# Recurrence of a two-layer hybrid decoder: paired level products, lanes that follow by an event, a shorter stated norm latency

## The chip, the cores and the metric

The kernel runs on one core of a Trainium2 chip. The core has five engines that matter here: TensorE (PE in the profile, with PEld for its weight loads), VectorE (DVE), ScalarE (ACT), GpSimd (POOL) and SyncE (SP), which issues the DMA transfers. Each engine works through its own instructions in order; semaphores let one wait for another. The metric is the device time of one execution in microseconds, as the median of several runs.

## The reference

Two decoder layers over 256 tokens of width 1024 in float32. Each layer adds to `x`, in this order, half a SwiGLU feed-forward block, a mixer, a cross attention over 256 memory tokens and another half feed-forward block, each behind an RMS norm. The mixer has two groups of heads side by side:

```python
z = h @ w_in                       # HGRN2 q|f|i|g, FoX q|k|v, forget logits
# HGRN2, 4 heads of 128: a gated linear recurrence
S_t = diag(f_t) S_{t-1} + (1 - f_t) i_t^T ;  o_t = S_t^T q_t
o_h = rms_norm(o_h, out_norm_w) * silu(g)
# FoX, 8 heads of 64: causal softmax attention with decaying bias
s = q k^T / 8 + (c_t - c_s),  c = cumsum(log sigmoid(ff + b))
o_f = softmax(s) v
x = x + concat(o_h, o_f) @ w_out
```

## The kernel before

**Precision and the large products.** Float32 results are built from three products of a fast 32-bit kind: high times high, high times low, low times high (`mm3`, lines 455 to 458). Activations and weights are split for that into a high and a low part: ScalarE casts the high part (`whi`, lines 159 and 163), VectorE subtracts it from the original for the low part (`wlo`, lines 160 and 164; `xfl`, `oTl`, `mfl`, line 383). Weights stream in by DMA in a fixed list of pieces of up to 1 MB (`raw`, three buffers), so TensorE's large matmuls, ScalarE's casts and VectorE's subtractions run side by side through the whole kernel. The large matmuls write the tiles `acc`, in four PSUM buffers; all small groups write tiles of one pool of four PSUM buffers (`smp`: ad, al, pc, mt, ax, ho, fs, fpt, fpv, hot, pt), taken in rotation.

**What sets the order.** The Python code of the kernel is a set of generators that `drive` runs against a virtual clock while the program is written. A generator that yields a number has used so much TensorE time; a tuple of one number means "not before so much later"; an `Event` means "not before it has been fired". The constants `LAT_...` state how long the other engines will take before TensorE's next step of that generator has its operands. So TensorE's order is fixed when the program is built, by these stated latencies; if one is too short, TensorE waits in order on a semaphore and everything behind it waits too. On ScalarE, VectorE and GpSimd a scheduler orders the instructions with priorities; some steps are raised (`high_priority`).

**The recurrence** (`hgrn`, lines 783 to 878) is worked out by doubling. Query and key (both [128 features, 4 heads, 256 tokens]; `q`, `qf = q*f`, `k`) meet first on the diagonal (`ad`), then on seven levels with blocks of 1, 2, 4 ... 64 tokens (`al`). A level multiplies k by qf in blocks (32 pairs of 32x32, 16 of 32x32 or 8 of 64x64; one pair shows as two matmuls in the trace). VectorE then takes the decays of the halves into the second half of qf (line 819) and the first half of k (line 821), both in place, works out the totals for the next level (line 825), and picks the level's entries out of PSUM into `Ac` by a mask (line 832). Levels 5 and 6 and the finished `Ac` are copied by ScalarE into the score matrix `A` (lines 829 and 836). After the last level come one product between the two halves of the tokens (`ax`, copied by ScalarE to `AX`, line 845), the outputs `ho` for the two token tiles (lines 855 and 856), and a norm per head: squares on ScalarE (line 863), sums on VectorE (line 865), a power on GpSimd (line 867), the scaling on VectorE (line 869, to `AX` for the first token tile and to `oh` for the second), and their transposes on TensorE (`hot`, line 875), split into `oTh` and `oTl`.

**The lanes.** Two generators `fox_lane` take two pairs of heads each. Per pair: `fox_stack` builds split queries and keys with the bias stacked in (`fqs`, `fks`, ScalarE's casts on lines 946 to 948), TensorE makes the scores (`fs`, line 967), VectorE adds the causal mask and takes the maximum, ScalarE the exponential (line 929), TensorE transposes the result (`fpt`, line 985), ScalarE copies it (`ppT`, line 988), and TensorE multiplies with v (`fpv`, lines 998 to 1000). The second lane's first pair is held 2.8 us of virtual time behind the first lane's.

**Around them** the main generator keeps writing large matmuls: the projections for FoX, the memory keys and values (`mfh`, `mfl`), then the output projection with the tiles `vc`, and the norm behind the mixer (`hn`, its inverse root on line 357, transposes `pt` on line 376), whose latency is stated as `LAT_X`.

Of the kernel before, what the change touches and what calls it, by code (L numbers as in the profile page):

```python
# [13 lines left out]
ALU = mybir.AluOpType  # L14
# [3 lines left out]
P = 128  # L18
# [16 lines left out]
TAIL = 6  # L35
HP = 100
LA_D, LA_S = 3, 1
LAT_NORM, LAT_X = 5.5, 6.5
LAT_LVL, LAT_AX, LAT_HN = 4.0, 1.5, 5.2
LAT_FS, LAT_FT, LAT_CQ, LAT_CS, LAT_CT = 7.0, 3.5, 2.6, 5.6, 3.0  # L40
LAT_Q, LAT_G1, LAT_G2, LAT_M = 5.0, 9.0, 2.0, 18.0
LAT_MEM = 42.0
LAT_FK, LAT_LANE = 6.5, 2.8

OFF_Q, OFF_F, OFF_I, OFF_G = 0, 512, 1024, 1536
OFF_FQ, OFF_FK, OFF_FV = 2048, 2560, 3072
# [3 lines left out]
def hymba_kernel(  # L50
# [6 lines left out]
    nc = tc.nc  # L57
# [26 lines left out]
    def smp(name="smp"):  # L84
        return pss.tile([P, 512], F32, name=nm(name), tag="smp")
# [328 lines left out]
    def spawn(gen):  # L414
        tasks.append([gen, clock[0], None])
# [365 lines left out]
    def hgrn(q, f, k, v, gw, oT, masks, ready, done):  # L781
        yield ready
        masks, eye = masks
        A2 = s4([P, NT, 4, P], F32, "A")
        A = [A2[:, t] for t in range(NT)]
        nc.gpsimd.memset(A2, 0.0)
        Ac = sm.tile([P, 8, 32], F32, name=nm("Ac"), tag="Ac", bufs=1)
        qf = s4([P, 4, S], F32, "qf")
        nc.vector.tensor_tensor(out=qf, in0=q, in1=f, op=ALU.mult)

        def blocks(ps, rhs, hb, step):

            for t in range(NT):
                for h in range(4):
                    c0 = (4 * t + h) * hb
                    for s0 in range(0, P, hb + step):
                        a = t * P + s0
                        nc.tensor.matmul(ps[s0:s0 + hb, c0:c0 + hb], lhsT=k[:, h, a:a + hb],  # L798
                                         rhs=rhs[:, h, a + step:a + step + hb], start=True, stop=True)

        ps = smp("ad")
        blocks(ps, q, 32, 0)
        nc.vector.tensor_tensor(out=Ac, in0=ps[:, 0:256].rearrange("p (g t) -> p g t", g=8),
                                in1=eye.unsqueeze(1).to_broadcast([P, 8, 32]), op=ALU.mult)
        yield 1.3
        tots = s4([P, 1024], F32, "tots")
        tot = f.rearrange("p h t -> p (h t)")
        qflat = qf.rearrange("p h t -> p (h t)")
        kflat = k.rearrange("p h t -> p (h t)")
        for lv in range(7):  # L810
            hb = 1 << lv
            ps = smp("al")
            blocks(ps, qf, max(32, hb), hb if lv >= 5 else 0)
            nb = 4 * S // (2 * hb)
            tv = tot.rearrange("p (b two) -> p b two", two=2)
            qv = qflat.rearrange("p (b two j) -> p b two j", two=2, j=hb)
            kv = kflat.rearrange("p (b two j) -> p b two j", two=2, j=hb)
            with tc.high_priority(offset=HP):
                nc.vector.tensor_tensor(out=qv[:, :, 1, :], in0=qv[:, :, 1, :],
                                        in1=tv[:, :, 0:1].to_broadcast([P, nb, hb]), op=ALU.mult)  # L820
                nc.vector.tensor_tensor(out=kv[:, :, 0, :], in0=kv[:, :, 0, :],
                                        in1=tv[:, :, 1:2].to_broadcast([P, nb, hb]), op=ALU.mult)
                if lv < 6:
                    nt_ = tots[:, 1024 - 2 * nb:1024 - nb]
                    nc.vector.tensor_tensor(out=nt_, in0=tv[:, :, 0], in1=tv[:, :, 1], op=ALU.mult)
                    tot = nt_
            if lv >= 5:
                for s0 in range(0, P, 2 * hb):
                    nc.scalar.copy(out=A2[s0:s0 + hb, :, :, s0 + hb:s0 + 2 * hb],
                                   in_=ps[s0:s0 + hb, 0:8 * hb].rearrange("p (t h j) -> p t h j", t=NT, h=4))  # L830
            else:
                nc.vector.copy_predicated(Ac, masks[:, lv, :].unsqueeze(1).to_broadcast([P, 8, 32]),
                                          ps[:, 0:256].rearrange("p (g t) -> p g t", g=8))
            if lv == 4:
                for s0 in range(0, P, 32):
                    nc.scalar.copy(out=A2[s0:s0 + 32, :, :, s0:s0 + 32],
                                   in_=Ac[s0:s0 + 32].rearrange("p (t h) j -> p t h j", t=NT))
            yield 1.3 if lv < 5 else 0.8
            yield (LAT_LVL,)
        ps = smp("ax")  # L840
        for h in range(4):
            nc.tensor.matmul(ps[:, h * P:(h + 1) * P], lhsT=k[:, h, 0:P], rhs=qf[:, h, P:S], start=True, stop=True)
        AX2 = s4([P, 2, 4, P], F32, "AX")
        AX_ = AX2[:, 0]
        nc.scalar.copy(out=AX_, in_=ps.rearrange("p (h t) -> p h t", h=4))
        yield 4 * 0.213
        yield (LAT_AX,)
        oT.alloc(0)
        ohs = []
        for t in range(NT):  # L850
            po = smp("ho")
            for h in range(4):
                o = po[:, h * P:(h + 1) * P]
                if t == 1:
                    nc.tensor.matmul(o, lhsT=AX_[:, h, :], rhs=v[:, 0, h * P:(h + 1) * P], start=True, stop=False)
                nc.tensor.matmul(o, lhsT=A[t][:, h, :], rhs=v[:, t, h * P:(h + 1) * P], start=t == 0, stop=True)
            yield (4 + 4 * t) * 0.213
            oh_ = AX2[:, 1] if t == 0 else s4([P, 4, P], F32, "oh")
            ohs.append(oh_)
            pv = po.rearrange("p (h e) -> p h e", h=4)  # L860
            ss = small(4, "hss")
            for h in range(4):
                nc.scalar.activation(oh_[:, h, :], pv[:, h, :], AF.Square, scale=float(P) ** -0.5,
                                     accum_out=ss[:, h:h + 1])
            nc.vector.tensor_scalar(out=ss, in0=ss, scalar1=EPS, scalar2=None, op0=ALU.add)
            rs = small(4, "hrs")
            nc.gpsimd.tensor_tensor(out=rs, in0=ss, in1=neghalf, op=ALU.pow)  # L867
            for h in range(4):
                nc.vector.scalar_tensor_tensor(out=oh_[:, h, :], in0=pv[:, h, :], scalar=rs[:, h:h + 1],
                                               in1=gw[:, t, h * P:(h + 1) * P], op0=ALU.mult, op1=ALU.mult)  # L870
        yield (LAT_HN,)
        for t in range(NT):
            pt = smp("hot")
            for h in range(4):
                nc.tensor.transpose(pt[:, h * P:(h + 1) * P], ohs[t][:, h, :], ident)
            sl = slice(t * P, (t + 1) * P)
            put_split(oT.h[0][:, :, sl], oT.l[0][:, :, sl], pt.rearrange("p (k t) -> p k t", k=4))
            yield 4 * T1
        done.fire(1.6)
# [74 lines left out]
                                    scalar2=None, op0=ALU.mult)  # L954
        return qs, ks

    def fox_lane(lane, fq, fk, fv, L_, R_, oT, cmask, oh, ready, done):
        yield ready
        for pr in (lane, lane + 2):
            qs, ks = fox_stack(pr, fq, fk, L_, R_, oh)  # L960
            yield (LAT_FK + LAT_LANE * (pr == 1),)
            prs = []
            for sub in range(2):
                ps = smp("fs")
                for t, o, n in SEGS:
                    for j in range(2):
                        nc.tensor.matmul(ps[:, o:o + n], lhsT=qs[:, j, sub, t * P:(t + 1) * P], rhs=ks[:, j, sub, 0:n],
                                         start=j == 0, stop=j == 1)
                yield 0.44
                pr_ = pp()  # L970
                prs.append(pr_)
                mx = small(2, "fmx")
                for t, o, n in SEGS:
                    nc.vector.tensor_tensor_reduce(out=pr_[:, o:o + n], in0=ps[:, o:o + n], in1=cmask[:, S - n:S],
                                                   scale=1.0, scalar=-3.0e38, op0=ALU.add, op1=ALU.max,
                                                   accum_out=mx[:, t:t + 1])
                nmx = small(2, "fnm")
                nc.vector.tensor_scalar(out=nmx, in0=mx, scalar1=-1.0, scalar2=None, op0=ALU.mult)
                softmax(pr_, nmx, 1.0, [(t, pr_[:, o:o + n], pr_[:, o:o + n]) for t, o, n in SEGS])
            yield (LAT_FS,)  # L980
            pTs = []
            for sub in range(2):
# [9 lines left out]
            for sub in range(2):  # L992
                h = 2 * pr + sub
# [16 lines left out]
    def mixer(cur, l, consts, nxt_w):  # L1010
# [57 lines left out]
            nc.scalar.copy(out=fv[:, t, 0:260], in_=ps[t][:, 0:260])  # L1068
        oT.alloc(1)
        ev_p = [Event() for _ in range(4)]  # L1070
        for lane in range(2):
            spawn(fox_lane(lane, fq, fk, fv, L_, R_, oT, cmask, oh, ev_g, ev_p))
        kc = [[s4([P, 4, S], F32R, "kc") for _ in range(2)] for _ in range(2)]
        yield ev_m
        for c in range(2):
# [180 lines left out]
```

## Time and profile before

| | before |
|---|---|
| median of 3 runs | 1209.25 us (1209.22 to 1209.48) |
| profiled execution | 1209.23 us |
| span of its instructions | 1207.4 us |
| granted TensorE clock | 0.999 |
| busy: TensorE / VectorE / ScalarE / GpSimd | 99% / 64% / 54% / 3% of the span |
| DMA, mean over the span | 181 GB/s |

The profile is one execution. Busy shares are taken of the span, which leaves out 1.8 us at the execution's ends. Matmuls are pipelined: their recorded durations overlap, so the distance between two starts says what one costs, and the idle times in the list of waits say where TensorE had nothing to do. In the timeline's rows the bracket gives the idle time before the row and what ended it.

### The profile page before, as it was taken

How to read it: one execution, taken by the hardware profiler on the slowest of the kernel's cores; microseconds unless marked ns; L12 is line 12 of the kernel's file. 1: busy time of each engine (PE TensorE's matmuls, PEld its weight loads, DVE VectorE, ACT ScalarE, POOL GpSimd, SP SyncE). 2: the span in 40 equal slices, each digit the busy share in tenths (PEclk: the TensorE clock that was granted, in tenths of full speed). 3: DMA queues.
4: the chain of work that ended last, by engine and by line, in shares of the span. 5: the costliest groups of instructions: out<-in, count | busy, mean ns of one | idle time of the engine just before them, and what ended most of it. 6: DMA issues, size and time to landing. Idle time of an engine off the chain costs nothing.

```text
span 1207.4 us, 21487 instructions
## 1 busy us (share of the span) xinstructions
PE 1194.0 (99%) x8989; PEld 1095.0 (91%) x8989; DVE 769.1 (64%) x1194; ACT 651.2 (54%) x1022; POOL 36.7 (3%) x50
## 2 busy tenths in 40 slices
PE   9999999999999999999999999999999999999997
PEld 7999888999889889998889998889988898999986
DVE  6866647578866675565474565476787766555643
ACT  7565735568854454444354454266686555444532
POOL 0000000001000000000000000000110000000000
PEclk9999999999999999999999999999999999999999
DMA  8655755544544374566474566464445533555750
GB/s 300 217 195 179 273 183 174 168 136 140 180 152 175 105 262 154 195 212 207 140 261 141 209 210 209 140 227 159 149 150 174 191 128 136 194 192 175 245 174 36
DMA packets 100001, 218.66 MB, mean 181 GB/s; under 512 B 4128, under 2 KB 16704, under 8 KB 99904
## 3 DMA queue, kind: packets, MB, share of 16 engines
q1 hardware_dynamic: 99744, 217.03, 53.1%
q8 instruction: 70, 1.15, 0.4%
q10 hardware_dynamic: 160, 0.27, 0.1%
q14 instruction: 27, 0.22, 0.1%
HBM read 216.23 MB, written 1.05 MB: 180 GB/s over the span
## 4 chain that ended last, share of the span: by engine, by line
PE 88%; DVE 5%; ACT 3%; issue 2%; POOL 1%; DMA 0%; POOLq 0%; ACTq 0%
PE acc L456 27%; PE acc L458 27%; PE acc L457 27%; DVE wlo L164 1%; DVE wlo L160 1%; ACT whi L163 1%; PE acc L521 1%; PE pt L376 1%; POOL rs L357 1%; PE al L798 1%; DVE xfl L383 0%; ACT pp L929 0%; POOL hrs L867 0%; PE cpo L457 0%; PE cpo L456 0%
## 5 line engine op out<-in xcount | busy, mean ns | idle before, releaser
L160 DVE TENSOR_TENSOR wlo<-raw,whi 128x1024 fp32r<-128x1024 f32 (+1 forms) x332 | 389.5, 1197 | 251.8 <-ACT whi L159 243.3
L159 ACT CAST whi<-raw 128x1024 fp32r<-128x1024 f32 (+1 forms) x332 | 331.9, 1029 | 256.6 <-PE acc L458 144.7
L456 PE MATMUL acc<-xfh,whi 128*128 128x256 f32 x1536 | 425.5, 277 | 1.0 <-issue 1.0
L457 PE MATMUL acc<-xfl,whi 128*128 128x256 f32 x1536 | 424.3, 276 | 0.7 <-DVE xfl L383 0.7
L458 PE MATMUL acc<-xfh,wlo 128*128 128x256 f32 x1536 | 424.1, 276 | 0.0
L457 PEld LDWEIGHTS acc<-xfl,whi 128*128 128x128 f32 x1536 | 288.3, 188 | 2.5 <-DVE xfl L383 1.1
L456 PEld LDWEIGHTS acc<-xfh,whi 128*128 128x128 f32 x1536 | 288.4, 188 | 0.8
L458 PEld LDWEIGHTS acc<-xfh,wlo 128*128 128x128 f32 x1536 | 288.3, 188 | 0.0
L456 PE MATMUL acc<-whi,hth 128*128 128x512 f32 (+1 forms) x352 | 137.0, 389 | 0.0
L458 PE MATMUL acc<-whi,htl 128*128 128x512 f32 (+1 forms) x352 | 136.4, 387 | 0.0
L457 PE MATMUL acc<-wlo,hth 128*128 128x512 f32 (+1 forms) x352 | 136.3, 387 | 0.0
L456 PE MATMUL acc<-whi,xfh 128*128 128x512 f32 (+1 forms) x240 | 87.5, 365 | 0.0
L458 PE MATMUL acc<-whi,xfl 128*128 128x512 f32 (+1 forms) x240 | 86.9, 362 | 0.0
L457 PE MATMUL acc<-wlo,xfh 128*128 128x512 f32 (+1 forms) x240 | 86.6, 361 | 0.0
L458 PEld LDWEIGHTS acc<-whi,htl 128*128 128x128 f32 x352 | 66.1, 188 | 13.6
L456 PEld LDWEIGHTS acc<-whi,hth 128*128 128x128 f32 x352 | 66.1, 188 | 13.3
L457 PEld LDWEIGHTS acc<-wlo,hth 128*128 128x128 f32 x352 | 66.1, 188 | 13.3
L164 DVE SCALAR_TENSOR_TENSOR wlo<-raw,g,whi 128x512 fp32r<-128x512 f32 (+1 forms) x96 | 62.1, 702 | 19.7 <-ACT whi L163 19.7
L163 ACT ACTIVATE whi<-raw,g 128x512 fp32r<-128x512 f32 (+1 forms) x96 | 58.3, 677 | 18.0 <-PE acc L457 15.0
L458 PEld LDWEIGHTS acc<-whi,xfl 128*128 128x128 f32 x240 | 45.1, 188 | 7.2
L457 PEld LDWEIGHTS acc<-wlo,xfh 128*128 128x128 f32 x240 | 45.1, 188 | 6.9
L456 PEld LDWEIGHTS acc<-whi,xfh 128*128 128x128 f32 x240 | 45.1, 188 | 6.8
(274 smaller groups left out, 1498.2 us busy)
## 6 DMA issues: line engine op xcount, KB each, us to landing
raw<-in_ffn_w_down_dram SPq DMA_DIRECT2D x44, 1024.0 KB, 4.9
raw<-in_ffn_w_up_dram SPq DMA_DIRECT2D x40, 1024.0 KB, 5.5
raw<-in_ffn_w_gate_dram SPq DMA_DIRECT2D x38, 1024.0 KB, 5.2
raw<-in_w_in_dram SPq DMA_DIRECT2D x24, 1024.0 KB, 5.3
raw<-in_cross_wk_dram SPq DMA_DIRECT2D x8, 1024.0 KB, 5.6
raw<-in_cross_wv_dram SPq DMA_DIRECT2D x8, 1024.0 KB, 5.3
raw<-in_w_out_dram SPq DMA_DIRECT2D x8, 1024.0 KB, 5.0
raw<-in_cross_wq_dram SPq DMA_DIRECT2D x8, 1024.0 KB, 5.1
```

The lines of the kernel that those rows point to most:

```text
L159: nc.scalar.copy(out=hi, in_=sl)
L160: nc.vector.tensor_tensor(out=lo, in0=sl, in1=hi.bitcast(F32), op=ALU.subtract)
L163: nc.scalar.mul(hi, sl, g)
L164: nc.vector.scalar_tensor_tensor(out=lo, in0=sl, scalar=g, in1=hi.bitcast(F32), op0=ALU.mult, op1=ALU.subtract)
L357: nc.gpsimd.tensor_tensor(out=rs, in0=ms, in1=neghalf[:, 0:1], op=ALU.pow)
L376: nc.tensor.transpose(pt[:, j * P:(j + 1) * P], hn[:, kt * P:(kt + 1) * P], ident)
L456: nc.tensor.matmul(ps, lhsT=lh, rhs=rh, start=start, stop=False)
L457: nc.tensor.matmul(ps, lhsT=lh, rhs=rl, start=False, stop=False)
L458: nc.tensor.matmul(ps, lhsT=ll, rhs=rh, start=False, stop=stop)
L521: nc.tensor.matmul(psa_[t], lhsT=x, rhs=w, start=kt == 0 and which == 0, stop=kt == KT - 1 and which == 1)
L798: nc.tensor.matmul(ps[s0:s0 + hb, c0:c0 + hb], lhsT=k[:, h, a:a + hb], rhs=rhs[:, h, a + step:a + step + hb], start=True, stop=True)
```

## The change

- Level 1 and level 3 of the recurrence are held: their products are issued together with those of level 2 and level 4, as one burst into two halves of one PSUM tile. The held level's operands must stay as they are until then, so its updated query and key go to a spare pair of tiles (`q` and `f`, which are done with by then, and back). VectorE writes the changed halves there, and ScalarE copies the unchanged halves: two more copies at each held level.
- Level 0's products go into the second half of the diagonal's tile. The two groups stood next to each other before.
- The wait after a held level is stated as `LAT_LV2` = 7.0, and level 0 and 2 lead straight on to the held level's updates.
- The second lane no longer follows by a fixed wait. The first lane fires an event behind the softmax of its first pair, with a latency of 1.9, and the second lane waits for it before its scores.
- `LAT_X`, stated for the norm behind the mixer, goes from 6.5 to 5.3.

```diff
-LAT_NORM, LAT_X = 5.5, 6.5
+LAT_NORM, LAT_X = 5.5, 5.3
+LAT_LV2 = 7.0
...
-LAT_FK, LAT_LANE = 6.5, 2.8
+LAT_FK, LAT_LANE = 6.5, 1.9
...
-        def blocks(ps, rhs, hb, step):
+        def blocks(ps, k, rhs, hb, step):
...
         ps = smp("ad")
-        blocks(ps, q, 32, 0)
...
-        yield 1.3
+        blocks(ps, k, q, 32, 0)
...
+        old, spare = [], (q, f)
         for lv in range(7):
             hb = 1 << lv
-            ps = smp("al")
-            blocks(ps, qf, max(32, hb), hb if lv >= 5 else 0)
+            held = lv in (1, 3)
+            pend = [] if held else old + [(lv, k, qf)]
+            lvs = []
+            if lv and not held:
+                ps = smp("al")
+            for l_, k_, q_ in pend:
+                part = ps[:, 256:512] if l_ in (0, 2, 4) else ps
+                blocks(part, k_, q_, max(32, 1 << l_), hb if lv >= 5 else 0)
+                lvs.append((l_, part))
...
+            qv, kv = halves(qf), halves(k)
+            if held:
+                old, (qf, k), spare = [(lv, k, qf)], spare, (qf, k)
+            else:
+                old = []
+            qn, kn = halves(qf), halves(k)
             with tc.high_priority(offset=HP):
-                nc.vector.tensor_tensor(out=qv[:, :, 1, :], in0=qv[:, :, 1, :],
+                nc.vector.tensor_tensor(out=qn[:, :, 1, :], in0=qv[:, :, 1, :],
                                         in1=tv[:, :, 0:1].to_broadcast([P, nb, hb]), op=ALU.mult)
-                nc.vector.tensor_tensor(out=kv[:, :, 0, :], in0=kv[:, :, 0, :],
+                nc.vector.tensor_tensor(out=kn[:, :, 0, :], in0=kv[:, :, 0, :],
                                         in1=tv[:, :, 1:2].to_broadcast([P, nb, hb]), op=ALU.mult)
+                if held:
+                    nc.scalar.copy(out=qn[:, :, 0, :], in_=qv[:, :, 0, :])
+                    nc.scalar.copy(out=kn[:, :, 1, :], in_=kv[:, :, 1, :])
...
-            yield 1.3 if lv < 5 else 0.8
-            yield (LAT_LVL,)
+            if held:
+                yield (LAT_LV2,)
+            else:
+                yield 0.7 * (len(lvs) + (lv == 0)) if lv < 5 else 0.8
+                yield (LAT_LVL if lv not in (0, 2) else 0.0,)
...
     def fox_lane(lane, ..., ready, done, ahead):
...
-            yield (LAT_FK + LAT_LANE * (pr == 1),)
+            yield (LAT_FK,)
+            if pr == 1:
+                yield ahead
...
+            if pr == 0:
+                ahead.fire(LAT_LANE)
             yield (LAT_FS,)
```

More of the change, by code (lines that the diff above doesn't have):

```diff
@@ L801, in hgrn @@
         ps = smp("ad")
-        blocks(ps, q, 32, 0)
-        nc.vector.tensor_tensor(out=Ac, in0=ps[:, 0:256].rearrange("p (g t) -> p g t", g=8),
-                                in1=eye.unsqueeze(1).to_broadcast([P, 8, 32]), op=ALU.mult)
-        yield 1.3
+        blocks(ps, k, q, 32, 0)
         tots = s4([P, 1024], F32, "tots")
         tot = f.rearrange("p h t -> p (h t)")
-        qflat = qf.rearrange("p h t -> p (h t)")
-        kflat = k.rearrange("p h t -> p (h t)")
+        old, spare = [], (q, f)
@@ L814, in hgrn, with halves @@
             nb = 4 * S // (2 * hb)
             tv = tot.rearrange("p (b two) -> p b two", two=2)
-            qv = qflat.rearrange("p (b two j) -> p b two j", two=2, j=hb)
-            kv = kflat.rearrange("p (b two j) -> p b two j", two=2, j=hb)
+            def halves(x):
+                return x.rearrange("p h t -> p (h t)").rearrange("p (b two j) -> p b two j", two=2, j=hb)
+            qv, kv = halves(qf), halves(k)
[3 more added lines that the diff above has]
+                old = []
@@ L831, in hgrn @@
             else:
-                nc.vector.copy_predicated(Ac, masks[:, lv, :].unsqueeze(1).to_broadcast([P, 8, 32]),
-                                          ps[:, 0:256].rearrange("p (g t) -> p g t", g=8))
+                if lv == 0:
+                    nc.vector.tensor_tensor(out=Ac, in0=ps[:, 0:256].rearrange("p (g t) -> p g t", g=8),
+                                            in1=eye.unsqueeze(1).to_broadcast([P, 8, 32]), op=ALU.mult)
+                for l_, part in lvs:
+                    nc.vector.copy_predicated(Ac, masks[:, l_, :].unsqueeze(1).to_broadcast([P, 8, 32]),
+                                              part[:, 0:256].rearrange("p (g t) -> p g t", g=8))
             if lv == 4:
@@ L955, in fox_stack, with fox_lane @@
         return qs, ks
-    def fox_lane(lane, fq, fk, fv, L_, R_, oT, cmask, oh, ready, done):
+    def fox_lane(lane, fq, fk, fv, L_, R_, oT, cmask, oh, ready, done, ahead):
         yield ready
@@ L1070, in mixer @@
         ev_p = [Event() for _ in range(4)]
+        ahead = Event()
         for lane in range(2):
-            spawn(fox_lane(lane, fq, fk, fv, L_, R_, oT, cmask, oh, ev_g, ev_p))
+            spawn(fox_lane(lane, fq, fk, fv, L_, R_, oT, cmask, oh, ev_g, ev_p, ahead))
         kc = [[s4([P, 4, S], F32R, "kc") for _ in range(2)] for _ in range(2)]
```

## The prediction

> **What bounds the kernel now.** I read the profile's page first, then the list of TensorE's waits, then the timeline of TensorE through both mixers, and last the timelines of ScalarE and VectorE beside it. The page says which engine sets the time (first its busy line, then the chain that ended last, by engine):
>
> ```profile
> PE 1194.0 (99%) x8989; PEld 1095.0 (91%) x8989; DVE 769.1 (64%) x1194; ACT 651.2 (54%) x1022; POOL 36.7 (3%) x50
> ...
> PE 88%; DVE 5%; ACT 3%; issue 2%; POOL 1%; DMA 0%; POOLq 0%; ACTq 0%
> ```
>
> TensorE is busy for 1194.0 of a span of 1207.4 us. VectorE (64%) and ScalarE (54%) have room on the average. So time can come from only two places: holes in TensorE's row, and the price of each small group of matmuls that stands between the large ones. The profiled execution took 1209.23 us, 1.8 us more than its span; the median of the runs is 1209.25, so sums made on the span carry over.
>
> The holes, from the list of TensorE's waits (us in total, times, longest):
>
> ```profile
> PE fs L967 <- DVE AX L869: 1.0, 1, 1.0
> PE acc L456 <- issue: 1.0, 1, 1.0
> PE fpt L985 <- DVE oTl L383: 0.8, 1, 0.8
> PE acc L457 <- DVE xfl L383: 0.7, 2, 0.4
> PE acc L458 <- DVE wlo L164: 0.5, 1, 0.5
> PE pt L376 <- DVE hn L370: 0.4, 2, 0.2
> PE fpv L998 <- ACT ppT L988: 0.3, 1, 0.3
> ```
>
> These seven add to 4.7 us. Five of them (fs, issue, fpt, wlo, fpv: 3.6) lie inside a mixer, and xfl (0.7) right behind each. That is about all that better placing can win.
>
> The price of a small group is read at the recurrence of layer 1, on TensorE's timeline (start, us, engine, line, operation; "x64" is one level's burst):
>
> ```profile
> 242.43 0.28 PE L458 MATMUL acc<-whi,xfl 128*128 128x260 f32 x1
> 242.64 0.73 PE L798 MATMUL ad<-hq,kk 128*32 128x32 f32 x62
> ...
> 243.23 0.74 PE L798 MATMUL al<-qf,kk 128*32 128x32 f32 x62
> 243.90 0.39 PE L456 MATMUL acc<-xfh,whi 128*128 128x256 f32 x1
> 244.12 0.28 PE L457 MATMUL acc<-xfl,whi 128*128 128x256 f32 x1
> ...
> 244.92 0.28 PE L458 MATMUL acc<-xfh,wlo 128*128 128x256 f32 x1
> 246.21 0.28 PE L456 MATMUL acc<-xfh,whi 128*128 128x256 f32 x1 [1.01 <-issue]
> 246.32 0.28 PE L457 MATMUL acc<-xfl,whi 128*128 128x256 f32 x1
> ...
> 249.62 0.28 PE L458 MATMUL acc<-xfh,wlo 128*128 128x256 f32 x1
> 249.83 0.76 PE L798 MATMUL al<-qf,kk 128*32 128x32 f32 x64
> 250.52 0.39 PE L456 MATMUL acc<-xfh,whi 128*128 128x256 f32 x1
> 250.75 0.28 PE L457 MATMUL acc<-xfl,whi 128*128 128x256 f32 x1
> ```
>
> Large matmuls of 256 columns start 0.115 us apart. A level alone takes from 249.62 to 250.75, 1.13 us with two such steps in it, so 0.90. "ad" and the first level back to back take from 242.43 to 244.12, 1.69, less 0.23 is 1.46. The second burst thus costs 0.56 instead of 0.90: **a join saves 0.34, and each break of two neighbours costs about as much**.
>
> **The change part by part.** *Joins.* The small groups on TensorE in layer 1, in program order, before (ad and al are the bursts of the levels, pc the gates' prefix sum, mt the transposes of mem; large matmuls stand at each mark):
>
> ```order
> L798 MATMUL ad_2631<-hq_2429,kk_2298 32x32 x32
> L798 MATMUL al_2666<-qf_2629,kk_2298 32x32 x32
> ...
> L798 MATMUL al_2779<-qf_2629,kk_2298 32x32 x32
> ...
> L908 MATMUL pc_2854<-tri,lf_2740 128x256 x2
> L798 MATMUL al_2857<-qf_2629,kk_2298 32x32 x32
> L1120 MATMUL mt_2894<-ident,mem_1992 128x128 x4
> ```
>
> and with the change:
>
> ```order
> L799 MATMUL ad_2631<-hq_2429,kk_2298 32x32 x32
> L799 MATMUL ad_2631<-qf_2629,kk_2298 32x32 x32
> ...
> L799 MATMUL al_2812<-qf_2629,kk_2298 32x32 x32
> L799 MATMUL al_2812<-hq_2429,fg_2297 32x32 x32
> ...
> L799 MATMUL al_2988<-hq_2429,fg_2297 32x32 x32
> L799 MATMUL al_2988<-qf_2629,kk_2298 32x32 x32
> L1149 MATMUL mt_3062<-ident,mem_2003 128x128 x4
> ```
>
> "ad" and level 0 were neighbours already. Levels 1 and 2 join (0.34) and 3 and 4 join (0.34), but level 2 had stood beside pc and mt, and leaves them (one break back). Net one join a layer: 2 x -0.34 = **-0.7**. Nothing (0) would be the end if bursts in two halves of one tile cost as two; 2 x -0.68 = -1.4 the other.
>
> *Copies.* A held level writes its updated operands to spare tiles, which adds two ScalarE copies of 128x512, at 2 levels in 2 layers 8 copies. The nearest row, and ScalarE's room where they fall in layer 1 (the window's busy time of each engine):
>
> ```profile
> L1124 ACT COPY mem_t<-mt 128x512 f32<-128x512 f32 x4 | 2.4, 602 | 2.3 <-DVE mfl L383 2.3
> 246.00:262.00 16.00, 15.79 (x304) 15.02 (x304) 11.42 (x26) 8.41 (x16) 0.00 (x0) 1.00 0.20 52
> ```
>
> ScalarE is idle for 7.6 of those 16 us, so 4 x 0.6 = 2.4 are hidden there behind the large matmuls: **0**. Without that cover each pair would hold a burst back by 1.2, 4.8 in all. VectorE's updates are as large as they were.
>
> *Norm behind the mixer.* The stated latency falls from 6.5 to 5.3, so its transposes, and the split that VectorE does from them, are issued earlier. The wait to be won (layer 1; VectorE, then TensorE):
>
> ```profile
> 359.95 5.76 DVE L160 TENSOR_TENSOR wlo<-raw,whi 128x1024 fp32r<-128x1024 f32 x5
> 365.62 1.28 DVE L383 TENSOR_TENSOR xfl<-pt,xfh 128x512 fp32r<-128x512 f32 x2
> 366.36 0.39 PE L457 MATMUL acc<-xfl,whi 128*128 128x256 f32 x1 [0.34 <-DVE xfl L383]
> ```
>
> xfl stands in VectorE's queue behind five weight splits; asked for 1.2 us earlier it passes one. I take the 0.7 of both layers as gone: **-0.7**. Not more, and not below 0 to +0.7, should the transposes now wait for hn as they do for 0.4 above.
>
> *Lanes, layer 2.* Before, ho and the scores of both lanes (fs) stood in one block:
>
> ```profile
> 884.92 1.17 PE L967 MATMUL fs<-fks,fqs 128*128 128x128 f32 x8
> 887.14 1.28 PE L967 MATMUL fs<-fks,fqs 128*128 128x128 f32 x8 [1.05 <-DVE AX L869]
> ...
> 896.92 1.14 PE L985 MATMUL fpt<-ident,pp 128*128 128x128 f32 x6 [0.81 <-DVE oTl L383]
> ```
>
> Now 12 large matmuls follow ho, then lane 0, then 18 more, then lane 1 (TensorE, layer 2, end of the recurrence):
>
> ```order
> L880 MATMUL ho_9555<-hv_8329,A_8836 128x128
> ...
> L993 MATMUL fs_9589<-fks_9451,fqs_9450 128x128 x2
> ...
> L993 MATMUL fs_9643<-fks_9467,fqs_9466 128x128 x2
> L993 MATMUL fs_9643<-fks_9467,fqs_9466 128x256 x2
> L993 MATMUL fs_9661<-fks_9467,fqs_9466 128x128 x2
> ...
> L899 MATMUL hot_9685<-ident,AX_9519 128x128 x4
> L899 MATMUL hot_9692<-ident,oh_9564 128x128 x4
> ```
>
> So fs of lane 1 comes 12 x 0.115 + 1.0 + 18 x 0.115 = 4.5 us after ho, past the VectorE step that frees its bank (AX): -1.05. fpt (0.81) and wlo (0.5) move apart in the same way: -1.3. Small excesses beside these (in the two blocks quoted, 0.1 to 0.3 each): -0.6. Against it stand four breaks (ho|fs, fs|fs, and two where the products with v no longer pair) at 0.34: +1.3. And a new wait: the second half of lane 1 (fs_9661) takes the bank of ho's second half, freed only when VectorE has read it for oh, which I put at 7.6 us behind ho against 7.1 + 0.5 for the matmul; with ScalarE's copy of AX up to 0.7 late, +1.1 (0 to 2). Layer 2: -1.05 - 1.3 - 0.6 + 1.3 + 1.1 = **-0.6**.
>
> *Lanes, layer 1.* The rows of before (group rows of ScalarE's casts for the lanes; then single rows of three engines at the end of the recurrence):
>
> ```profile
> L946 ACT CAST fqs<-fq 64x512 fp32r<-64x512 f32 x16 | 9.9, 616 | 0.2
> L948 ACT CAST fks<-fk 64x256 fp32r<-64x256 f32 x16 | 6.5, 405 | 0.4
> 282.83 1.05 PE L842 MATMUL ax<-qf,kk 128*128 128x128 f32 x8
> 285.75 1.05 PE L856 MATMUL ho<-hv,A 128*128 128x128 f32 x8
> 286.05 0.56 ACT L845 COPY AX<-ax 128x512 f32<-128x512 f32 x1
> 287.75 0.26 ACT L863 ACTIVATE AX<-ho 128x128 f32<-128x128 f32 x1
> 293.16 1.13 DVE L869 SCALAR_TENSOR_TENSOR oh<-ho,hrs,gw 128x128 f32<-128x128 f32 x4 [0.93 <-POOL hrs L867]
> 294.34 0.66 PE L875 MATMUL hot<-ident,AX 128*128 128x128 f32 x4
> 294.90 0.66 PE L875 MATMUL hot<-ident,oh 128*128 128x128 f32 x4
> ```
>
> From the first square (287.75) to the end of oh (294.29) is 6.5 us; hot's second transpose needs oh. Before, the casts of both lanes were done ahead of AX's copy. With the change ScalarE has, in layer 1:
>
> ```order
> L869 COPY AX_3257<-ax_3252 128x512
> L970 CAST fqs_3279<-fq_2713 64x2x256
> ...
> L971 CAST fks_3296<-fk_2937 64x256
> L972 CAST fks_3296<-fk_2937 64x256
> L887 ACTIVATE AX_3257,hss_3350<-ho_3345 128x128 x4
> L887 ACTIVATE oh_3371,hss_3372<-ho_3362 128x128 x4
> ```
>
> Twelve casts and two copies of fv now stand between AX's copy and the squares: 4 x (0.62 + 2 x 0.40) less their overlap of about 0.1 each, and 0.5, is some 6 us. ax and ho come about 3.5 us sooner (27 large matmuls fewer ahead of them, and the join), near 279.4 and 282.3; AX's copy, no longer kept back to 286.05 by other work, starts 1.1 behind ax and ends near 281, so the squares start near 287 and oh ends near 293.3. TensorE reaches hot's second half after ho (2.7), 36 large ones (4.1), fs (1.0), 6 large (0.7) and hot's first half (0.5), at 291.3 to 292: a new wait of **+1.5** (1.0 to 2.2). Two breaks (ho|fs and one pair of products with v): +0.7. Gone are fpv's 0.3 and some 0.3 in the blocks: -0.6. Layer 1: **+1.6**.
>
> **Fetch.** The 1.01 at 246.21 is "issue": TensorE had operands and no instruction. The page's row of the instruction queue:
>
> ```profile
> q8 instruction: 70, 1.15, 0.4%
> ```
>
> 70 packets for 8989 matmuls are 128 matmuls (with their weight loads) a packet. A double burst of 128 uses a packet up in 1.26 us, where large matmuls take 128 x 0.115 = 14.7. Before, each layer had one double burst, and one of the two starved, which cost 1.29 - 0.12 = 1.17 over the step. Now there are three a layer; the old one keeps its place. I take **0** for the four new ones, since starving needs the burst to meet a packet's end while the next is late, which no rule of this program steers; the bound is 4 x 1.17 = +4.7. [...]
>
> Sum: joins -0.7, norm -0.7, layer 2 -0.6, layer 1 +1.6, others 0: -0.4, so 1209.2 - 0.4 = **1208.8 us**. A difference under 0.2% (2.4 us) can't be told from no change here.
>
> **Rivals.** *The new waits don't come (faster).* If ScalarE's casts finish in the shadow of the large matmuls, +1.5 and +1.1 fall away: 1208.8 - 2.6 = 1206.2. For it: ScalarE is idle nearly half the time, and every old hole has its row. Against: in layer 1 its queue order puts the casts ahead of the squares.
>
> *The double bursts starve (slower).* Place: the large matmuls just behind levels 1|2 and 3|4; price 1.17 each, all four: 1208.8 + 4.7 = 1213.5. From the third on it is slower than 1211.7. For it: one of two did; against: the list shows one "issue" in the span, though the same burst ran in layer 2. One alone gives 1210.0, inside no change.
>
> *The change doesn't do what it says.* Two halves of one tile from different operands cost two full groups: no join, +0.7, 1209.5.
>
> *The lanes' queue is worse.* If each cast waits for VectorE's subtraction behind it, the four groups take 0.5 more each, and hot waits 2 us longer: 1210.8.
>
> **How the numbers follow.** Chances: forecast 0.42 (1207.4 to 1210.2), no new waits 0.26, starving 0.10 (half of it with one or two bursts), no join 0.10, lanes' queue 0.12. Faster by over 0.2% (below 1206.8): most of the second case and a little of the first, 0.24. Slower (above 1211.7): half the third and a part of the last, 0.12. No change: 0.64. The range: from 1206.2, less a little for joins at their full 1.4, so 1205.9, up to 1210.8 and a part of a starved burst, 1211.4.
>
> **What would show it.** The changed kernel's waits of TensorE: hot <- oh in layer 1 at 1 to 2 us says the queue of casts is as told, none says the rival; fs <- AX and fpt <- oTl gone, fs <- oh under 1 in layer 2; no acc <- xfl; bursts of x126 or more at three places a layer, 1.46 each; "issue" once and 1.0, a second one is the starved burst. I am wrong if a wait over 2 us stands anywhere else in a mixer.

## The result, and the profile after

The changed kernel takes 1213.03 us (median of 6 runs, 1211.90 to 1216.62) against 1209.11 (6 runs, 1208.46 to 1209.48): a ratio of 1.004, 95% interval 1.0029 to 1.0051. It is slower by 3.9 us; 1208.8 with a range of 1205.9 to 1211.4 was forecast. The profiled execution took 1215.45, with a span of 1213.6.

The busy line of the changed kernel's page, then its list of TensorE's waits:

```profile
PE 1197.6 (99%) x8989; PEld 1098.9 (91%) x8989; DVE 770.4 (63%) x1194; ACT 655.6 (54%) x1030; POOL 32.6 (3%) x50
```

```profile
PE hot L899 <- DVE oh L893: 2.1, 1, 2.1
PE acc L458 <- issue: 1.7, 1, 1.7
PE ho L879 <- ACT AX L869: 1.6, 1, 1.6
...
PE hot L899 <- DVE AX L893: 0.9, 1, 0.9
PE acc L457 <- issue: 0.8, 1, 0.8
...
PE fs L993 <- DVE oh L893: 0.4, 1, 0.4
```

The old waits of fs on AX, of fpt, xfl, wlo and fpv are gone, as forecast. New are hot with 3.0 us (layer 1), a second issue wait of 1.7 (layer 1) and ho with 1.6 (layer 2). TensorE is also "busy" 3.6 us longer with the same 8989 matmuls, so some of them ran slower. The windows of 1 us at the end of layer 1's recurrence show where (after a window's bounds and length come the busy times of TensorE, its weight loads, VectorE, ScalarE and GpSimd, then the granted clock, the DMA share and GB/s):

```profile
297.00:298.00 1.00, 0.00 (x0) 0.00 (x0) 0.95 (x4) 0.00 (x0) 0.82 (x4) 0.55 0.00 0
298.00:299.00 1.00, 0.77 (x5) 0.77 (x5) 1.00 (x9) 0.00 (x0) 0.78 (x2) 0.50 0.00 0
...
303.00:304.00 1.00, 1.00 (x6) 1.00 (x6) 0.95 (x6) 0.61 (x3) 0.00 (x0) 0.53 0.00 0
304.00:305.00 1.00, 1.00 (x11) 1.00 (x10) 1.00 (x6) 0.16 (x1) 0.00 (x0) 1.00 0.00 0
```

While TensorE waited for oh, the granted clock fell from 1.00 to 0.50, and it stayed there until 303.9. Six matmuls fall into the microsecond from 303, eleven into the next: the large ones of 256 columns start 0.21 us apart up to 303.9 and 0.12 behind it. In the profile of before the clock is 1.00 through both mixers.

To see which part of the program pays, I took from each trace the start times of the same matmuls, counted in order without those on constants: the 100th, the 2860th (behind the mixer of layer 1), and the 6080th and 7380th (around the mixer of layer 2). The stretches between them, in us:

| kernel | up to the 100th | to the 2860th, with mixer 1 | mixer 2 | the rest | span |
|---|---|---|---|---|---|
| before | 28.5 | 340.0 | 130.9 | 708.0 | 1207.4 |
| changed | 30.6 | 346.0 | 129.2 | 707.8 | 1213.6 |

The stretch with mixer 1 lost 6.0 us and mixer 2 won 1.7, together 4.3, close to the 3.9 of the medians. The 2.1 at the start are no work of the change: in every profiled execution here the first matmuls run at half pace, and for how long differs from one to the next. At 10 to 11 us the large matmuls of 512 columns start 0.23 us apart in the execution of before, at 11 to 12 still 0.43 in that of the changed kernel (TensorE's timeline of before, then of the changed kernel):

```profile
10.34 0.40 PE L521 MATMUL acc<-whi,xfl 128*128 128x512 f32 x1
10.57 0.40 PE L521 MATMUL acc<-whi,xfh 128*128 128x512 f32 x1
```

```profile
11.31 0.63 PE L522 MATMUL acc<-whi,xfl 128*128 128x512 f32 x1
11.74 0.63 PE L522 MATMUL acc<-whi,xfh 128*128 128x512 f32 x1
```

The two losses of layer 1, in the changed kernel's timelines. The first stands behind the joined burst of levels 3 and 4 (TensorE):

```profile
265.89 0.28 PE L457 MATMUL acc<-xfh,whi 128*128 128x256 f32 x1
267.91 0.39 PE L458 MATMUL acc<-xfl,whi 128*128 128x256 f32 x1 [1.74 <-issue]
```

The second is hot (rows of TensorE, ScalarE and VectorE, in order of time):

```profile
283.17 1.05 PE L866 MATMUL ax<-qf,kk 128*128 128x128 f32 x8
285.24 0.57 ACT L869 COPY AX<-ax 128x512 f32<-128x512 f32 x1
285.70 0.62 ACT L970 CAST fqs<-fq 64x512 fp32r<-64x512 f32 x1
...
291.32 0.41 ACT L972 CAST fks<-fk 64x256 fp32r<-64x256 f32 x1
291.63 0.27 ACT L887 ACTIVATE AX<-ho 128x128 f32<-128x128 f32 x1
295.47 0.66 PE L899 MATMUL hot<-ident,AX 128*128 128x128 f32 x4 [0.92 <-DVE AX L893]
297.05 1.13 DVE L893 SCALAR_TENSOR_TENSOR oh<-ho,hrs,gw 128x128 f32<-128x128 f32 x4 [0.90 <-POOL hrs L891]
298.23 1.12 PE L899 MATMUL hot<-ident,oh 128*128 128x128 f32 x4 [2.10 <-DVE oh L893]
```

The queue of casts is as told: 5.9 us from the first cast (285.70) to the first square (291.63), and 6.55 from there to the end of oh (298.18).

### The profile page after: what moved, and what is told of

Its sections match the earlier page's. It is cut to its first block, busy times and chain, and to the rows that moved or that the text cites. A ratio compares the mean times of both kernels' runs of the same rounds, so it can differ in the third digit from the quotient of the medians.

```text
span 1213.6 us, 21506 instructions
## 1 busy us (share of the span) xinstructions
PE 1197.6 (99%) x8989; PEld 1098.9 (91%) x8989; DVE 770.4 (63%) x1194; ACT 655.6 (54%) x1030; POOL 32.6 (3%) x50
## 3 DMA queue, kind: packets, MB, share of 16 engines
q8 instruction: 70, 1.15, 0.4%
HBM read 216.23 MB, written 1.05 MB: 179 GB/s over the span
## 4 chain that ended last, share of the span: by engine, by line
PE 93%; ACT 2%; DVE 2%; issue 2%; DMA 1%; POOL 1%; POOLq 0%; ACTq 0%; DVEq 0%
PE acc L457 28%; PE acc L458 28%; PE acc L459 28%; PE acc L522 1%; PE pt L377 1%; PE fs L993 1%; DVE wlo L165 0%; PE al L799 0%; DMA raw<-in_cross_wk_dram 0%; PE fpt L1013 0%; ACT whi L164 0%; POOL hrs L891 0%; PE cpo L458 0%; PE cpo L457 0%; PE cpo L459 0%
## 5 line engine op out<-in xcount | busy, mean ns | idle before, releaser
L383 ACT CAST hth<-sil 128x512 fp32r<-128x512 f32 x36 | 22.3, 619 | 53.7 <-DVE sil L762 53.7
```

Of the source, the lines that this page charges most:

```text
L383: nc.scalar.copy(out=hi, in_=src)
```

## The experiments

Theory: (a) the pairing brings ho forward on TensorE, ScalarE has the lanes' casts between AX's copy and the squares, so hot waits; (b) the idle time brings the clock down for a while; (c) a joined burst that uses up an instruction packet starves. The rivals: the event of the lanes holds hot back; the clock falls because of the bursts; the issue wait belongs to a burst wherever its packet ends.

The same stretches as above, each from the one profiled execution of a kernel (us; the first column only varies with the slow start and with padding), and the medians, each set beside the kernel before on the same chips:

| kernel | to the 100th | to the 2860th | mixer 2 | median | ratio to before, 95% |
|---|---|---|---|---|---|
| before | 28.5 | 340.0 | 130.9 | 1208.7 to 1209.1 | |
| changed | 30.6 | 346.0 | 129.2 | 1213.03 | 1.0040 (1.0029, 1.0051) |
| pairing only | 28.8 | 347.8 | 130.3 | 1214.12 | 1.0048 (1.0033, 1.0063) |
| lanes only | 28.0 | 340.0 | 131.7 | 1209.95 | 1.0007 (0.9998, 1.0017) |
| hot later | 28.6 | 344.5 | 130.5 | 1211.98 | 1.0027 (1.0017, 1.0037) |
| squares raised | 30.6 | 344.2 | 129.4 | 1214.22 | 1.0048 (1.0033, 1.0063) |
| before, padded | 28.6 | 338.8 | 130.9 | 1208.02 | 0.9991 (0.9982, 1.0000) |
| changed, padded | 28.5 | 341.1 | 129.4 | 1208.59 | 0.9998 (0.9988, 1.0008) |
| start 7.0 | 28.0 | 339.9 | 129.6 | 1207.34 | 0.9985 (0.9976, 0.9995) |
| start 8.5 | 28.2 | 338.1 | 132.3 | 1208.26 | 0.9997 (0.9987, 1.0006) |
| start 8.5 and 7.0 | 28.0 | 338.4 | 129.5 | 1206.74 | 0.9984 (0.9975, 0.9994) |
| the same, padded | 28.4 | 338.1 | 129.5 | 1205.69 | 0.9972 (0.9962, 0.9982) |
| before, hot earlier | 28.9 | 342.1 | 131.0 | 1211.64 | 1.0027 (1.0015, 1.0039) |

**Pairing alone.** The changed kernel with the lanes and the norm's latency as before:

```diff
-LAT_NORM, LAT_X = 5.5, 5.3
+LAT_NORM, LAT_X = 5.5, 6.5
-LAT_FK, LAT_LANE = 6.5, 1.9
+LAT_FK, LAT_LANE = 6.5, 2.8
...
-            yield (LAT_FK,)
-            if pr == 1:
-                yield ahead
+            yield (LAT_FK + LAT_LANE * (pr == 1),)
```

> Only the pairing of levels; lanes and norm latency as before. Theory (pairing moves ho ahead of the casts on ScalarE in layer 1; hot then waits 3 us, the clock falls for some 6 us, and one double burst starves): 3 us of hot waits, a granted clock under 0.999, a second issue wait of 1 to 2 us; 1212 to 1214 us. Rival (the event of the lanes is what holds hot back): no hot wait over 1 us, 1208.5 to 1210.5 us.

1214.12 us. Three rows of its list of TensorE's waits:

```profile
PE hot L899 <- DVE oh L893: 2.1, 1, 2.1
PE acc L458 <- issue: 1.8, 1, 1.8
PE hot L899 <- DVE AX L893: 1.6, 1, 1.6
```

The whole loss of layer 1 is here without the lanes' event, and the clock stands at 0.50 from 296.7 to 303.5. The wait of acc on xfl stands at 0.7 as before; with the shorter norm latency of the full change it is gone.

**The lanes alone**, the event and 1.9 put into the kernel before:

> Only the event of the lanes with 1.9; levels and norm latency as before. Theory (pairing is the cause): no hot wait, one issue wait of 1.0, clock 0.999, within 1 us of before: 1208 to 1210. Rival (the event is the cause): hot waits 2 us or more, 1211 to 1214.

1209.95 us, no hot wait, no difference in layer 1 (340.0). In layer 2 it loses 0.8. The list of TensorE's waits there:

```profile
PE acc L458 <- DVE wlo L164: 1.2, 2, 0.7
PE acc L456 <- ACT whi L163: 0.8, 1, 0.8
```

The waits of fs and fpt went, and the large matmuls now wait for their weights instead: by itself the event moves the time, and wins none.

**Hot later**, the changed kernel with the scores of lane 1 ahead of hot:

```diff
-LAT_LVL, LAT_AX, LAT_HN = 4.0, 1.5, 5.2
+LAT_LVL, LAT_AX, LAT_HN = 4.0, 1.5, 9.0
```

> The changed kernel with the latency stated ahead of hot raised from 5.2 to 9.0, so that hot stands behind the scores of lane 1. Theory (the two hot waits of 3.0 us in sum and the lower clock behind them are one cost): hot waits under 0.5, granted clock 1.00 in every window of the mixer, 4.5 to 5.5 us less than the changed kernel: 1207.5 to 1209. Rival (the clock falls by itself, for instance from the bursts): the waits go but the clock still falls, 1210 to 1211.

1211.98: the expectation missed. Two of its waits, then a window behind the second issue wait:

```profile
PE fs L993 <- DVE oh L893: 2.4, 2, 2.1
PE acc L458 <- issue: 1.9, 1, 1.9
```

```profile
267.00:268.00 1.00, 1.00 (x7) 1.00 (x6) 0.00 (x0) 0.39 (x1) 0.00 (x0) 0.50 0.12 31
```

Hot waits no more, but the scores of lane 1 stand in its place: their PSUM bank is that of ho's second half, which VectorE frees with oh. So it is oh that is late, whoever asks for it. And here the clock fell behind the issue wait of 1.9 instead, from 266.9 to 270.4, and not behind the 2.1 of fs. So a wait of about 2 us brought the clock down in one place here and not in the other; the windows of the last experiment show where the two fell.

**Squares raised**, the changed kernel with the norm's steps behind ho on ScalarE, VectorE and GpSimd at high priority:

```diff
+            with tc.high_priority(offset=HP):
+                ss = small(4, "hss")
+                for h in range(4):
+                    nc.scalar.activation(oh_[:, h, :], pv[:, h, :], AF.Square, ...
...
```

> The changed kernel with the norm steps behind ho raised in priority, so that on ScalarE the squares of the first token tile stand behind three of the lanes' casts instead of twelve, those of the second behind seven. TensorE's order is unchanged. Theory (the casts ahead of the squares make hot late): hot waits fall from 3.0 to under 0.7, clock 1.00, 1207.5 to 1209.5. Rival (hot waits for something else: GpSimd's power, VectorE's queue): hot waits stay over 2 us, 1212 to 1214.

1214.22 us, so the time did not follow, though the cause showed. Two of its waits:

```profile
PE fs L994 <- DVE fmx L1001: 1.5, 1, 1.5
PE hot L900 <- DVE oh L894: 0.9, 1, 0.9
```

Hot's waits fell from 3.0 to 0.9, a little short of the 0.7 expected: where these steps stand in the engines' queues sets them. The edit raised VectorE's and GpSimd's steps too, so ScalarE's share is not shown by this run alone. But the casts that were passed, and the steps on VectorE, now came late for lane 1, whose scores waited 1.5 for VectorE's maximum of lane 0, and from 300.3 to 303.7 the clock stood at 0.50 again. The stretch with mixer 1 is only 1.8 shorter than in the changed kernel, and the medians, taken on different chips, don't show even that.

**Packets shifted.** 32 matmuls of 32x32 on constants at the start of the kernel before (64 in the trace, a half packet), and 16 in the changed kernel (a quarter):

```diff
+    def pad(n):
+        for i in range(n):
+            s0 = 32 * (i % 4)
+            nc.tensor.matmul(warm[s0:s0 + 32, 0:32], lhsT=ident[:, s0:s0 + 32], rhs=ident[:, 0:32], ...
...
         warm_up(9)
+        pad(32)
```

> The kernel before with 32 extra 32x32 matmuls (64 in the trace) on constants at the start, which shift the ends of the instruction packets by half a packet against the bursts. Theory (a double burst uses up a packet while the next is late): the issue wait of 1.0 is gone, at a start longer by about 0.8 us; 1208 to 1209. Rival (the wait belongs to the burst itself): the issue wait stays at 1.0, 1209 to 1210.

> The changed kernel with 16 such extra matmuls at the start (a quarter of a packet). Theory: both issue waits (1.7 and 0.8) gone or under 0.5, the hot waits of 3.0 and the fall of the clock behind them stay; 1210 to 1212. Rival: both issue waits stay, 1212.5 to 1215.

Before, padded: 1208.02; no issue wait is left in its list, and the stretch with mixer 1 is 1.2 shorter. The changed kernel, padded: 1208.59, below the 1210 to 1212 expected; both issue waits are gone from its list. Its hot waits and a window behind them:

```profile
PE hot L906 <- DVE oh L900: 2.1, 1, 2.1
PE hot L906 <- DVE AX L900: 0.5, 1, 0.5
```

```profile
292.39:295.81 3.42, 3.37 (x16) 3.37 (x17) 2.52 (x12) 2.19 (x4) 0.61 (x2) 0.50 0.00 0
```

Neither burst was touched, only where the packets end against them, so these issue waits (1.0 in the kernel before, 1.7 and 0.8 in the changed one) hang on that. The count agrees: in the changed kernel the two waits lie 384 matmuls apart, three packets of 128, and so they do in the three other kernels that have both. The clock falls here too, but for 3.4 us (292.4 to 295.8), against 6.8 in the changed kernel (297.1 to 303.9; both ends from the trace's record of the granted clock). The two stretches differ by 4.9: 2.5 of issue waits, 0.4 of hot waits and an estimated 1.7, half of 3.4, for the clock come to 4.6. That the fall is shorter is not shown to be the padding's work.

**The recurrence stated to start later**, which puts the casts ahead of AX's copy on ScalarE again: `LAT_Q` 5.0 becomes 7.0, and 8.5.

> The changed kernel with the recurrence stated to start 2 us later (7.0 instead of 5.0), by which ScalarE gets the lanes' casts ahead of AX's copy again. Packets still end inside bursts that use them up in about 3 us of TensorE's time. Theory: hot waits under 1 us, issue waits of 1 to 2 us in sum still there, clock 1.00 at the end of the recurrence; 1208 to 1210.5. Rival (hot waits because the recurrence is shorter, whatever ScalarE's order): hot waits of 2 us or more, 1211 to 1214.

> The same with 8.5: the casts stand ahead of AX's copy, and no packet in the mixer of layer 1 is used up in under 4 us. Theory: no hot wait over 0.5, no issue wait over 0.5, clock 0.999; 1204.5 to 1207.5, faster than before. Rival (new waits come in their place): 1208 or more.

With 7.0, 1207.34 us, faster than before. Its waits in layer 1, then ScalarE around AX's copy:

```profile
PE fs L993 <- DVE oh L893: 0.9, 1, 0.9
PE ad L799 <- DVE qf L790: 0.6, 1, 0.6
PE acc L459 <- DVE wlo L165: 0.5, 1, 0.5
PE ho L879 <- ACT AX L869: 0.4, 1, 0.4
```

```profile
281.37 0.40 ACT L972 CAST fks<-fk 64x256 fp32r<-64x256 f32 x1
285.40 0.57 ACT L869 COPY AX<-ax 128x512 f32<-128x512 f32 x1
287.10 0.27 ACT L887 ACTIVATE AX<-ho 128x128 f32<-128x128 f32 x1
```

The last cast is 4 us ahead of the copy, the squares follow it by 1.7 us, hot waits no more, and the clock is 1.00 throughout. The pairing did not have to go for it. The expected issue waits did not come: by the count of 128 matmuls one packet was used up in 2.5 us and another in 3.3, and neither starved. With 8.5, where none in layer 1 was expected to be used up in under 4, one did:

```profile
PE al L799 <- issue: 1.1, 1, 1.1
```

So in these two runs a packet's length alone does not tell whether it starves. With 8.5 layer 1 is the best so far (338.1), but layer 2 loses 1.4 to waits for weights and for the lanes. The median of 1208.26 misses the 1204.5 to 1207.5 expected; the rival, new waits in place of the old, came.

**Both, by layer**, 8.5 in layer 1 and 7.0 in layer 2; and with packets shifted by half, three of the nine transposes at the start left out in exchange:

> The changed kernel with the recurrence stated to start at 8.5 in layer 1 and 7.0 in layer 2. Theory: the parts of the two runs add, layer 1 as with 8.5 (one issue wait of about 1 us left), layer 2 as with 7.0; 1204 to 1206.5, faster than before and than either. Rival (what is won in one layer is lost by another's timing): 1207 or more.

> The same with packet ends shifted by half a packet: 32 extra 32x32 matmuls at the start in place of three of the nine 128x128 transposes there. Theory: the last issue wait goes too, at a start up to 0.7 us longer; 1203.5 to 1206. Rival: as the run without the shift, or an issue wait at another burst.

1206.74 and 1205.69. By the stretches the parts add (338.4 and 129.5 in the first). The first median lies 0.2 above the range expected, over executions that spread from 1205.09 to 1208.21; what spreads them is not shown. The first trace has no issue wait, so the second can't show one going, and the 1.05 between the medians can't be put down to the packets. The second is 0.28% faster than before (ratio 0.9972, 0.9962 to 0.9982) and 7.3 us faster than the changed kernel. The one row of waits inside its mixers with a wait over 1 us:

```profile
PE acc L466 <- DVE wlo L165: 2.1, 2, 1.2
```

**The clock by itself.** The kernel before, levels unpaired, with only hot's latency lowered from 5.2 to 2.0:

> The kernel before, its levels unpaired, with only the latency ahead of hot lowered from 5.2 to 2.0, so that hot stands in front of the scores of lane 1 and waits for the norm. Theory (TensorE's idle time of 2.5 to 3.5 us within a few us brings the clock down, whatever brought the idle time): hot waits of 2.5 to 3.5 us in layer 1 and a granted clock near 0.5 for 3 to 6 us behind them, 1212 to 1215. Rival (the clock falls because of the paired bursts): the waits alone, clock 1.00, 1211 to 1212.

1211.64 us. Two waits, then two windows of its layer 1 and two of its layer 2:

```profile
PE hot L875 <- DVE oh L869: 2.5, 2, 1.5
...
PE hot L875 <- DVE AX L869: 0.4, 1, 0.4
```

```profile
289.93:293.34 3.41, 1.57 (x13) 1.13 (x11) 2.31 (x13) 1.11 (x1) 1.48 (x3) 1.00 0.64 240
293.34:296.75 3.41, 3.35 (x15) 3.13 (x16) 2.82 (x17) 2.36 (x10) 1.26 (x4) 0.50 0.00 0
887.26:890.68 3.42, 2.37 (x20) 2.14 (x20) 1.96 (x11) 2.90 (x10) 1.49 (x2) 1.00 0.20 72
890.68:894.09 3.41, 2.40 (x21) 2.05 (x20) 2.74 (x16) 1.44 (x7) 2.12 (x5) 1.00 0.00 0
```

In layer 1 hot waits 0.4 and 1.5, less than expected, and still the clock is at 0.50 from 293.3 to 296.8. The time lies in the rival's range, but the clock, which parts the two, did fall. No pairing, no new burst and no new issue wait is in this kernel (its one issue wait is 0.6): here the clock fell with idle time alone.

In each trace all changes of the clock lie a whole multiple of 3.413 us apart: in the changed kernel it rises at 13.80, falls at 297.10, rises at 303.93 and falls at the end at 1211.88, steps of 83, 2 and 266 times 3.413; in the kernel before it rises at 7.61 and falls at 1205.69, 351 steps apart. The windows above are cut at these changes and at multiples of 3.413 from them. Where the cuts fall in the program differs from execution to execution. Along them, three windows of the changed kernel, then two of hot later:

```profile
293.69:297.10 3.41, 1.52 (x12) 1.08 (x10) 1.91 (x7) 2.03 (x5) 2.03 (x3) 1.00 0.01 2
297.10:300.52 3.42, 2.29 (x11) 2.29 (x12) 3.42 (x16) 1.12 (x2) 1.56 (x4) 0.50 0.00 0
300.52:303.93 3.41, 3.41 (x18) 3.41 (x18) 1.75 (x11) 3.08 (x10) 0.00 (x0) 0.50 0.00 0
294.25:297.66 3.41, 1.90 (x15) 1.52 (x13) 2.19 (x8) 2.92 (x4) 2.03 (x3) 1.00 0.01 2
297.66:301.08 3.42, 2.49 (x21) 2.52 (x22) 3.38 (x18) 1.73 (x7) 1.27 (x4) 1.00 0.00 0
```

In the mixers of the 13 traces each of the five windows in which TensorE was busy for 1.57 us or less is followed by half clock. Of six with 1.81 to 1.90, one is (squares raised) and five are not. Half clock goes on behind windows with 2.29 and 2.62 and ends behind those with 3.35 or more. So in these mixers the clock fell with the idle time in one such window: each time at 1.84 us or more, once in six at 1.51 to 1.60. The 2.1 us of fs in hot later were split by a cut and cost no clock, like the 2.1 us of idle time in layer 2 of this run; the changed kernel's waits reached into a second window, and it paid twice. This also fits the spread of hot later's ten executions: 1210.50 us at a mean clock of 0.999 up to 1215.28 at 0.995.

## Why the prediction was wrong, by its own steps

The step that failed is layer 1: **+1.6** was forecast there, on top of one join (-0.35) and the norm (-0.35), so +0.9 in all; +6.0 was measured. Three terms make it up.

- *"a new wait of +1.5 (1.0 to 2.2)"* at hot was the right mechanism, too small: 3.0. The casts took the 6 us and the chain from squares to oh the 6.5 that I had reckoned. What was off is the start of that chain. "AX's copy ... starts 1.1 behind ax" was 2.07 (283.17 to 285.24), since ScalarE still split weights; so oh ended 12.3 us behind ho's start (285.84 to 298.18), where 11.0 was reckoned (282.3 to 293.3). TensorE reached hot 8.7 us behind ho's start (294.55, where hot's first wait begins), which with 0.5 for hot's first half agrees with the 9.0 to 9.7 reckoned to its second.
- *The clock was not in the sum at all.* From hot's second half (298.23) to 303.9 TensorE ran at a granted clock of 0.50, its large matmuls 0.21 us apart instead of 0.12: 5.7 us of which an estimated half, 2.8, is lost. I priced an idle microsecond at a microsecond. The kernel before with hot earlier shows the clock fall from idle time alone, and the changed kernel with the start at 7.0 shows it stay at 1.00 when the waits go.
- *Fetch, "I take 0 for the four new ones".* One of the four starved, for 1.7, as the rival of the double bursts priced one at 1.17; that rival, with all four, did not come. A shift of half a packet removes the wait from the kernel before, a quarter removes both from the changed one.

Together 3.0 + 2.8 + 1.7 less 0.2 (the old issue wait was shorter by that) are 7.3; the 6.0 leaves 1.3 for what the change won in layer 1: the joins, the waits of xfl and fpv, small excesses.

Right were: the joins (levels 1 and 2 as one burst cost 1.49 over the large matmuls, two alone 2 x 0.89, so a join saved 0.29); the copies, which no wait names; the norm, whose xfl waits of 0.7 are gone in the changed kernel and stand in the run without the shorter latency; the direction and nearly the size of layer 2 (-0.6, with join and norm -1.3; -1.7 measured), though its new waits came to 2.0 (ho on AX 1.6, fs on oh 0.4) where +1.1 (0 to 2) stood, the larger of them at a place that was not forecast, so the rest won more than I gave it: that the sum came close is luck in part. There the pairing alone gave -0.6 and the lanes alone +0.8; together with the shorter norm latency they gave -1.7.

*The lanes' queue* was a rival with 0.12, by casts that each wait for VectorE. They did not (0.62 and 0.40 as before, 5.9 us for all). The faster rival's condition, casts in the shadow, is what the later start of the recurrence brings about. The 1206.2 us that it forecast lie among the 1205.7 to 1208.3 measured for the four such kernels, which differ in more than that.

Half clock stands in the mixers of six kernels, for 3.4 or 6.8 us in each. The clock fell with waits of 0.4 and 1.5 us close together (before, hot earlier), and behind a single one of 1.9 (hot later).

The traces show when the next packet was fetched: its fetch is a transfer of 16 KB on the instruction queue (70 packets, 1.15 MB in the page's row). In all 12 issue waits of layer 1, over eight kernels, TensorE went on 1.2 to 1.5 us after such a fetch had ended; in the changed kernel the fetch ran from 265.56 to 266.63, and TensorE had nothing from 266.17 to 267.91. The kernels with the start at 8.5 and by layer have the same order of matmuls up to layer 2. In the one the fetch for the burst of levels 3 and 4 began at 264.01 and the burst starved for 1.1; in the other it began at 261.01 and nothing starved. So in these two the burst starved where the fetch of the next packet began 3.0 us later. Why it began late stays open: a weight transfer of 1 MB ran at about 400 GB/s ahead of the late fetch in the changed kernel, but in the by-layer kernel 373 GB/s ran from 261 to 262, where the fetch came in time.

## What to carry to other kernels

Put a price on TensorE's idle time that is higher than the time itself: where waits of about 2 us in sum fall into one window of 3.4 us, an estimated 1.7 to 2.8 us more were lost here at half clock, and where the windows lie differed from execution to execution. When a step on the critical engine is moved forward, look in the order of the engine that feeds it for what now stands in its way, and try moving the whole chain before taking the gain back; here a later start of the recurrence, stated by layer and with shifted packets, kept the pairing and turned 1213.0 into 1205.7 us. The bursts of very small matmuls met issue waits of 0.6 to 1.9 us here, and where a packet ends was one more thing that could be tuned.

## What was not expected of the hardware

- Granted clock 0.50 for 3.4 or 6.8 us behind 1.5 to 2.8 us of TensorE's idle time in one window of 3.41 us, in the middle of a kernel that is otherwise busy 99% of the time.
- The first matmuls run at half pace until 5.2 us in one execution (start at 7.0) and until 13.8 in the one of the changed kernel: 28.0 and 30.6 us up to the 100th matmul. That is 2.6 us of noise which no edit explains, and which a comparison by stretches leaves out.
- Issue waits of 0.6 to 1.9 us in layer 1 of eight kernels. 32 useless matmuls at the start removed that of the kernel before (1.0), 16 those of the changed one (1.7 and 0.8).
